# Row sums on every partition: a norm by one product on ones, a square root and a reciprocal of whole rows

## The chip, the cores and the metric

The kernel runs on one core of a Trainium2 chip. Its time is the device time of one execution in microseconds (us). Three executions of the kernel before took 1060.89, 1061.05 and 1061.98 us; the median is 1061.05 us. The engines are named as in the profile: PE is the matrix engine (TensorE), PEld its weight loads, DVE is VectorE, ACT is ScalarE, POOL is GpSimd, and SP issues DMAs. DMAs are issued from SP's and from ACT's queue. PSUM is the memory that PE writes its products to, SBUF the working memory.

## The reference

One inference step of a two-layer decoder trunk on 1056 tokens: 1024 of a prompt and 8 sequences of 4 sample tokens. Layer 0 is an RG-LRU block, layer 1 an HGRN2 block; each is a norm, an input projection, a mixer and an output projection that is added to the input. At the end stands one more norm. The change touches only how the norm is computed:

```python
def _rmsnorm(x, gain):
    xf = x.astype(jnp.float32)
    y = xf * lax.rsqrt(jnp.mean(xf * xf, axis=-1, keepdims=True) + EPS)
    return (y * gain.astype(jnp.float32)).astype(x.dtype)

# _trunk, shortened
for i in range(DEPTH):          # DEPTH = 2
    ...                         # layer 0: _lru_layer, layer 1: _hgrn_layer; each begins with _rmsnorm(x, g_norm)
return _rmsnorm(x, final_gain), ...
```

D_MODEL is 1024, EPS is 1e-6, and all is float32. The norm of x1 is the one at the entrance of layer 1, the final norm is the one in the last line.

## The kernel before

**Layout.** The tokens lie along the free dimension and the 1024 features along the partitions, in 8 blocks of 128 features. The sum of squares of a token is therefore a sum over partitions and over the 8 blocks. All large products are made of three products of parts (`mm3`, lines 243 to 245): each operand is split into a high and a low part, and high x high, high x low and low x high are added up in PSUM.

**Layer 0 and the norm of x1.** The tokens are cut into 3 chunks of 352. `out_last` computes the last part of layer 0's output projection, for each chunk 8 blocks m: a product on PE, an addition of the residual on DVE (line 698), a DMA, a square on ACT (line 430), and an addition of the square to an accumulator on POOL (line 433). After the 8 blocks of a chunk comes `norm`. It multiplies the accumulator, as weights, with a column of ones (`norm_sum`, line 277), three products of at most 128 tokens each, which leaves the sums with one token per partition. DVE scales them and adds EPS (line 445), POOL raises them to the power -0.5 (line 447), DVE makes a diagonal matrix of them (lines 448 and 451), and a product of a matrix of ones with that diagonal (line 453) brings the 352 factors as rows to all 128 partitions, in PSUM. `scaled_parts` multiplies each of the 8 blocks with its gain and with these rows (line 458, DVE), copies the high part (line 459, ACT) and subtracts it for the low part (line 323, DVE, or POOL for every fourth block). The first products of layer 1 (`first1`) read these parts: chunks 0 and 1 of two weight blocks first, chunk 2 of both last. Their first work on ACT is a Tanh (lines 714 and 718).

**The end of layer 1 and the final norm.** The output is finished in three pieces of 424, 376 and 256 tokens (`OUT`). For each piece and each of 8 blocks m: a product (9 matmuls), an addition on DVE (line 1724) that frees one of 3 PSUM banks, a square on ACT (line 1726), and for the first two pieces an addition to the accumulator on POOL (line 1735). Each piece's norm is worked off during the next piece: before block RM = 3 the sums (`summed`: `norm_sum`, then `roots` on DVE, POOL and DVE, lines 1664 to 1675), before block SM = 6 the product that spreads them (`spread`, line 1681) and then `finish`. `finish` multiplies each block with its gain and the factors. For the first piece DVE does all 8 blocks in one instruction each (line 1701), reading the factors from PSUM. For the others ACT copies the factors to SBUF (line 1694), ACT multiplies three blocks with the gain (line 1698) and POOL multiplies these with the copied factors (line 1699), while DVE does the other five from PSUM. Each block is written out by a DMA (line 310), in turn from SP's and ACT's queue.

For the last piece the sum over partitions is taken directly on PE: the accumulator of blocks 0 to 3 and then the squares of blocks 4 to 7 are each multiplied with the column of ones. Then come six products that nothing reads (line 1739), `roots`, `spread` and `finish`.

**What sets the order.** Each of the two layers collects all its instructions in a `Flow` with an engine, an estimated duration, what it reads and writes, and a priority. `Flow.run` plans the order of each engine's instructions from these estimates in turns, forwards and backwards, takes the best plan by its own estimate and writes the instructions in that order; for layer 0 a random search over the first 60 us is put on top. An instruction marked `both` is planned to wait for POOL where POOL is at work. So an edit of one instruction or one estimate can change the order elsewhere in the same layer. `hg` is a ring of PSUM banks, `xbs` a ring of three SBUF tiles of 384 columns.

Of the kernel before, what the change touches and what calls it, by code (L numbers as in the profile page):

```python
# [14 lines left out]
F32 = mybir.dt.float32  # L15
# [15 lines left out]
CUT = 2  # L31
SPOTS, SPOTS0, SPOTS1 = (6, 9, 0, 2), (2, 5, -1, -1), (1, 5, 9, 13, 17, 20)
K2 = 8 - K1
RM, SM = 3, 6
# [177 lines left out]
def tile_trunk(ctx: ExitStack, tc: tile.TileContext, xT, prm, hc, w0, wg, wo0, w1, wo1, s_in,  # L212
# [46 lines left out]
    smn = [0]  # L259

# [35 lines left out]
    with ExitStack() as l0:  # L296
# [18 lines left out]
        def dve(n, emit, r, w, prio=5, both=False):  # L315
            fl.add("DVE", 0.13 + 0.0011 * n, emit, r, w, prio, both=both)
# [118 lines left out]
        def norm(acc, own=None):  # L435
# [18 lines left out]
            return bc[:, :CH], bk  # L454

# [192 lines left out]
        def out_last(src):  # L648
# [42 lines left out]
            for c in range(NCH):  # L691
                acc = next(xbs)
                rows = []
                for i, m in enumerate(ms[c]):
                    ps, pk = product(blocks[m].get, ycols(c) + xcols(c)[:3], 1)
                    x, xk = spare[c][m]
                    dma(x, src[m][:, chunk(c)], ((2, m, c),), (xk,), 3)
                    dve(CH, lambda x=x, ps=ps: V.tensor_tensor(x, ps[:, :CH], x, op=ALU.add), (pk, xk), (xk,), 0)
                    dma(x1d[m][:, chunk(c)], x, (xk,), (("x1d", m, c),), 3)
                    squares(i, x, xk, acc)  # L700
                    rows.append((m, x, xk))
                bc, bk = norm(acc)
                for m, x, xk in rows:
                    scaled_parts(c, m, x, xk, bc, bk, pc("g1", m), ("P",), G if m % 4 == 3 else V, 4)
# [222 lines left out]
    with ExitStack() as l1:  # L927
# [728 lines left out]
        accs, sqs, dgs, sb = cycle(spare[:2]), cycle(spare[2:5]), cycle(spare[5:7]), spare[7]  # L1656
        nr2 = cycle([(fixed(f"nr2{i}", [128, 4], F32, p1), ("nr2", i)) for i in range(2)])

        def roots(n, sums, ready):

            r, rk = next(nr2)
            dg, dk = next(dgs)
            f, u = n // 128, n % 128
            dve(4, lambda: V.memset(r, 1.0), (), (rk,), 0)
            srcs = [(slice(i, i + 1), s[:w]) for i, (s, (_, w)) in enumerate(zip(sums, spans(n)))]
            for q, src in srcs:
                dve(4, lambda q=q, src=src: V.tensor_scalar(r[:src.shape[0], q], src, 1.0 / D, EPS, op0=ALU.mult, op1=ALU.add),
                    ready, (rk,), 0)
            w = len(srcs)
            fl.add("POOL", 0.85, lambda: G.tensor_tensor(r[:, :w], r[:, :w], mhalf[:, :w], op=ALU.pow), (rk,), (rk,), 0)  # L1670
            dve(128 * f, lambda: V.tensor_tensor(dg[:, :128 * f].rearrange("p (i n) -> p i n", i=f),
                                                 ident[:, None, :].to_broadcast([128, f, 128]),
                                                 r[:, :f, None].to_broadcast([128, f, 128]), op=ALU.mult), (rk,), (dk,), 0)
            if u:
                dve(u, lambda: V.tensor_scalar(dg[:, 128 * f:n], ident[:, :u], r[:, f:f + 1], None, op0=ALU.mult), (rk,), (dk,), 0)
            return dg[:, :n], dk

        def spread(n, dg, dk, main):

            bc, bk = next(hg)  # L1680
            fl.add("PE", 0.002 * n, lambda: T.matmul(bc[:, :n], ones, dg, start=True, stop=True), (dk,), (bk,), 0, main=main)
            return bc[:, :n], bk

        def summed(acc, ak, n):
            s, sk = next(hg)
            sums = [s[:, i:i + 1] for i in range(4)]
            fl.add("PE", 0.7, lambda: norm_sum(sums, acc, n, True, True), (ak,), (sk,), 0, main=True)
            return roots(n, sums, (sk,))

        def finish(a, n, bc, bk):  # L1690
            q = slice(a, a + n)
            own = KD - 3 if a else KD
            if a:
                act(n, lambda: S.copy(sb[0][:, :n], bc), (bk,), (sb[1],), 0)
            for k in (*range(own, KD), *range(own)):
                x, xk = x2[k][:, q], ykeys(Y2 + k, a, n)
                if k >= own:
                    act(n, lambda x=x, k=k: S.activation(x, x, AF.Copy, scale=pc("gf", k)), xk, xk, 1)
                    pool(n, lambda x=x: G.tensor_tensor(x, x, sb[0][:, :n], op=ALU.mult), (sb[1], *xk), xk, 1)
                else:  # L1700
                    dve(n, lambda x=x, k=k: V.scalar_tensor_tensor(x, x, pc("gf", k), bc, op0=ALU.mult, op1=ALU.mult), (bk, *xk), xk, 1)
                dma(yT[k][:, q], x, xk, (), 1, n / 2, S if k % 2 else Q)

        for a, n in OUT:
# [32 lines left out]
        spin, wk = next(mm)  # L1737
        for _ in range(6):
            fl.add("PE", 0.22, lambda: T.matmul(spin[:, :128], ones, ones, start=True, stop=True), sumk, (wk,), 0)
        finish(a, n, *spread(n, *roots(n, sums, sumk), False))  # L1740
# [72 lines left out]
```

## Time and profile before

| | |
|---|---|
| median of three runs | 1061.05 us (1060.89 to 1061.98) |
| the profiled execution: its own time | 1062.88 us |
| the profiled execution: its span, first to last instruction | 1061.1 us |
| mean granted TensorE clock | 0.995 |
| DVE busy | 843.7 us (80%) |
| ACT busy | 588.2 us (55%) |
| POOL busy | 542.0 us (51%) |

The profile comes from one execution. Every line of a timeline gives the start, the duration, the engine, the source line, the operation, the output and its inputs by the program's names, and the shape; a bracket gives idle time before it and who ended it. A line "x3" merges three instructions, and its duration is then that of the group. "PEclk" and "granted clock" give the clock that the matrix engine was granted, as a share of full speed. In the chain that ended last, a row is a piece of time that belongs to one engine and line, and the pieces do not overlap. An instruction's recorded duration includes a part that overlaps with its neighbour, so that two instructions in a row start closer together than one lasts.

### The profile page before, as it was taken

How to read it: one execution, taken by the hardware profiler on the slowest of the kernel's cores; microseconds unless marked ns; L12 is line 12 of the kernel's file. 1: busy time of each engine (PE TensorE's matmuls, PEld its weight loads, DVE VectorE, ACT ScalarE, POOL GpSimd, SP SyncE). 2: the span in 40 equal slices, each digit the busy share in tenths (PEclk: the TensorE clock that was granted, in tenths of full speed). 3: DMA queues.
4: the chain of work that ended last, by engine and by line, in shares of the span. 5: the costliest groups of instructions: out<-in, count | busy, mean ns of one | idle time of the engine just before them, and what ended most of it. 6: DMA issues, size and time to landing. Idle time of an engine off the chain costs nothing.

```text
span 1061.1 us, 25695 instructions
## 1 busy us (share of the span) xinstructions
PE 1051.4 (99%) x9972; PEld 1025.8 (97%) x9972; DVE 843.7 (80%) x1677; ACT 588.2 (55%) x1329; POOL 542.0 (51%) x604
## 2 busy tenths in 40 slices
PE   9999999999999999999999999999999999999997
PEld 9999999999999999999999999999999999999996
DVE  7999996888888689265799988978879797994435
ACT  6568656867675875243354474646464645652323
POOL 3425443444444455555677656555555565642544
PEclk9999999999999999999999999999999999999997
DMA  9201112123742685440210131312121212354204
GB/s 301 64 26 45 54 51 74 57 61 108 240 150 61 182 287 165 133 130 28 73 51 30 44 101 45 101 37 89 44 83 53 85 58 74 113 181 156 85 1 164
DMA packets 70121, 103.07 MB, mean 97 GB/s; under 512 B 9200, under 2 KB 51184, under 8 KB 70000
## 3 DMA queue, kind: packets, MB, share of 16 engines
q1 hardware_dynamic: 67696, 98.67, 29.9%
q10 hardware_dynamic: 2304, 2.77, 0.8%
q8 instruction: 78, 1.28, 0.5%
q14 instruction: 43, 0.35, 0.1%
HBM read 71.05 MB, written 25.49 MB: 91 GB/s over the span
## 4 chain that ended last, share of the span: by engine, by line
PE 89%; DVE 7%; POOL 1%; DMA 1%; issue 1%; ACT 0%; POOLq 0%; ACTq 0%; DVEq 0%
PE mm L243 24%; PE mm L244 24%; PE mm L245 24%; PE hg L567 1%; PE hg L1052 1%; PE hg L1161 1%; PE hg L1271 1%; DVE R L1368 1%; PE hg L1217 1%; PE hg L243 1%; PE hg L244 1%; PE hg L245 1%; PE hg L1273 1%; DMA wraw<-in_w_dram 1%; DVE tmp L1368 1%
## 5 line engine op out<-in xcount | busy, mean ns | idle before, releaser
L243 PE MATMUL mm<-xh,whi 128*128 128x352 f32 (+1 forms) x1143 | 358.8, 314 | 0.0
L245 PE MATMUL mm<-xh,wlo 128*128 128x352 f32 (+1 forms) x1143 | 353.4, 309 | 0.0
L244 PE MATMUL mm<-xl,whi 128*128 128x352 f32 (+1 forms) x1143 | 353.4, 309 | 0.0
L323 POOL TENSOR_TENSOR wlo<-wraw,whi 128x256 fp32r<-128x256 f32 (+3 forms) x184 | 203.2, 1121 | 178.7 <-ACT whi L378 79.9
L244 PEld LDWEIGHTS mm<-xl,whi 128*128 128x128 f32 x1143 | 215.3, 188 | 1.5
L243 PEld LDWEIGHTS mm<-xh,whi 128*128 128x128 f32 x1143 | 215.0, 188 | 1.5
L245 PEld LDWEIGHTS mm<-xh,wlo 128*128 128x128 f32 x1143 | 215.0, 188 | 0.0
L499 DVE SCALAR_TENSOR_TENSOR k<-xb,prm_sb,k 128x352 f32<-128x352 f32 (+2 forms) x144 | 90.0, 636 | 10.9 <-ACT k L496 7.7
L243 PE MATMUL mm<-t,whi 128*128 128x264 f32 (+1 forms) x306 | 89.4, 292 | 0.0
L244 PE MATMUL mm<-t,whi 128*128 128x264 f32 (+1 forms) x306 | 87.8, 287 | 0.0
L245 PE MATMUL mm<-t,wlo 128*128 128x264 f32 (+1 forms) x306 | 87.6, 286 | 0.0
L1501 DVE TENSOR_TENSOR k<-mm,k 128x264 f32<-128x264 f32 x144 | 60.2, 426 | 20.6 <-PE mm L245 17.5
L323 POOL TENSOR_TENSOR wlo<-R,whi 128x256 fp32r<-128x256 f32 x64 | 60.0, 957 | 24.7 <-ACT whi L1428 24.7
L582 POOL TENSOR_TENSOR k<-X 128x352 f32<-128x352 f32 x36 | 43.9, 1228 | 47.8 <-DVE R L583 38.2
L378 ACT CAST whi<-wraw 128x512 fp32r<-128x512 f32 (+2 forms) x83 | 46.1, 574 | 30.0 <-PE mm L244 15.7
L243 PEld LDWEIGHTS mm<-t,whi 128*128 128x128 f32 x306 | 57.7, 188 | 0.2
L245 PEld LDWEIGHTS mm<-t,wlo 128*128 128x128 f32 x306 | 57.8, 189 | 0.0
L244 PEld LDWEIGHTS mm<-t,whi 128*128 128x128 f32 x306 | 57.7, 189 | 0.0
L1428 ACT CAST whi<-wraw 128x512 fp32r<-128x512 f32 x52 | 32.1, 619 | 36.3 <-PE mm L245 16.8
L243 PE MATMUL mm<-yh,whi 128*128 128x352 f32 x153 | 50.0, 327 | 0.0
L245 PE MATMUL mm<-yh,wlo 128*128 128x352 f32 x153 | 49.4, 323 | 0.0
L244 PE MATMUL mm<-yl,whi 128*128 128x352 f32 x153 | 49.4, 323 | 0.0
(479 smaller groups left out, 2640.9 us busy)
## 6 DMA issues: line engine op xcount, KB each, us to landing
wraw<-in_w_dram SPq DMA_DIRECT2D x90, 256.0 KB, 2.8
wraw<-in_wo_dram SPq DMA_DIRECT2D x34, 192.0 KB, 2.6
si<-in_s_in_dram SPq DMA_DIRECT2D x8, 512.0 KB, 3.6
out_ss_out_dram<-si SPq DMA_DIRECT2D x8, 512.0 KB, 2.6
R<-in_w_dram SPq DMA_DIRECT2D x15, 256.0 KB, 2.6
sg<-x1b SPq DMA_DIRECT2D x21, 176.0 KB, 3.0
x<-sg SPq DMA_DIRECT2D x21, 176.0 KB, 1.9
R<-td SPq DMA_DIRECT2D x72, 44.0 KB, 2.0
```

Of the source, the lines that this page charges most:

```text
L243: T.matmul(out, wh, xh, start=first, stop=False)
L244: T.matmul(out, wh, xl, start=False, stop=False)
L245: T.matmul(out, wl, xh, start=False, stop=last)
L323: emit = lambda: e.tensor_tensor(b, x, a.bitcast(F32), op=ALU.subtract)
L378: act(m, lambda hi=hi, raw=raw, m=m: S.copy(hi[:, :m], raw[:, :m]), rk, (hk,), prio)
L499: dve(u, lambda src=src, dst=dst, sh=sh, k=k: V.scalar_tensor_tensor(dst, sh(src, k), pc("cw", 12 * k + m), dst, op0=ALU.mult, op1=ALU.add ...
L567: fl.add("PE", 0.62, lambda ps=ps, i=i, c=c: T.matmul(ps[:96, :CH], gs[:, i, :], ST[:96, chunk(c)], start=True, stop=True), (("gs",), *((" ...
L582: pool(CH, lambda x=x, a=a, b=b: G.tensor_tensor(x, a.bitcast(F32), b.bitcast(F32), op=ALU.add), (ak, bk), (xk,), 3)
L1052: T.matmul(ps[32 * j:32 * j + 32, n * w:n * w + w], B[:, o:o + 32], q(slice(o, o + 32)), start=True, stop=True, tile_position=(0, 32 * j))
L1368: dve(n, lambda: V.tensor_tensor(o, a, b, op=op), r, (w,), prio, True)
L1428: act(512, lambda: S.copy(hi, raw), (rk,), (hk,), 2)
L1501: dve(QT, lambda: V.tensor_tensor(o[0], z[0], u[0], op=ALU.add), (z[1], u[1]), (o[1],), 0)
```

## The change

For the norm of x1 (`norm_row` in place of `norm`, in `out_last` only; the first norm of layer 0 keeps `norm`) and for the final norm, the accumulator is now the moving operand of one product with a 128x128 matrix of ones. That leaves the sum of each token in every one of the 128 partitions, as a row in PSUM. ACT takes the square root of the whole row, with 1/D as scale and EPS as bias, and writes it to SBUF. DVE takes the reciprocal of the whole row in place. The scalings then read the factors from that SBUF row. The small products with a column of ones, the POOL power, the diagonal matrix and the product that spreads it go, and so do the ACT copy in `finish` and the six products that nothing reads. For the last piece the accumulator and the four squares are each multiplied with the matrix of ones, 256 columns wide. `finish` of a piece now follows its sums at once, before block 3; SM is gone. DVE's scalings in `finish` are marked `both`.

```diff
-RM, SM = 3, 6
+RM = 3
+TL = 1.3
...
+    epsc = const.tile([128, 1], F32, name="eps")
+    V.memset(epsc, EPS)
...
+        def norm_row(acc, o, ok):
+
+            a, ak = acc
+            ps, pk = next(hg)
+            fl.add("PE", 0.62, lambda: T.matmul(ps[:, :CH], ones, a[:, :CH], start=True, stop=True), (ak,), (pk,), 0)
+            act(CH, lambda: S.activation(o[:, :CH], ps[:, :CH], AF.Sqrt, bias=epsc, scale=1.0 / D), (pk,), (ok,), 0, TL)
+            dve(CH, lambda: V.reciprocal(o[:, :CH], o[:, :CH]), (ok,), (ok,), 0, more=1.2)
+            return o[:, :CH], ok
...
-                bc, bk = norm(acc)
+                bc, bk = norm_row(acc, *next(xbs))
...
+        def roots(n, ps, pk):
+
+            dg, dk = next(dgs)
+            act(n, lambda: S.activation(dg[:, :n], ps, AF.Sqrt, bias=epsc, scale=1.0 / D), (pk,), (dk,), 0)
+            fl.add("DVE", 0.13 + 0.0047 * n, lambda: V.reciprocal(dg[:, :n], dg[:, :n]), (dk,), (dk,), 0)
             return dg[:, :n], dk
...
         def summed(acc, ak, n):
             s, sk = next(hg)
-            sums = [s[:, i:i + 1] for i in range(4)]
-            fl.add("PE", 0.7, lambda: norm_sum(sums, acc, n, True, True), (ak,), (sk,), 0, main=True)
-            return roots(n, sums, (sk,))
+            fl.add("PE", 0.0018 * n, lambda: T.matmul(s[:, :n], ones, acc[:, :n], start=True, stop=True), (ak,), (sk,), 0, main=True)
+            return roots(n, s[:, :n], sk)
...
-            if a:
-                act(n, lambda: S.copy(sb[0][:, :n], bc), (bk,), (sb[1],), 0)
...
-                    pool(n, lambda x=x: G.tensor_tensor(x, x, sb[0][:, :n], op=ALU.mult), (sb[1], *xk), xk, 1)
+                    pool(n, lambda x=x: G.tensor_tensor(x, x, bc, op=ALU.mult), (bk, *xk), xk, 1)
                 else:
-                    dve(n, lambda x=x, k=k: V.scalar_tensor_tensor(x, x, pc("gf", k), bc, op0=ALU.mult, op1=ALU.mult), (bk, *xk), xk, 1)
+                    dve(n, lambda x=x, k=k: V.scalar_tensor_tensor(x, x, pc("gf", k), bc, op0=ALU.mult, op1=ALU.mult), (bk, *xk), xk, 1, True)
...
                 if a and m == RM:
-                    dg = summed(*prev[:2], prev[3])
-                if a and m == SM:
-                    finish(*prev[2:], *spread(prev[3], *dg, True))
+                    finish(*prev[2:], *summed(*prev[:2], prev[3]))
...
                     if m == 4:
-                        sums = [(next(hg)) for _ in spans(n)]
-                        sumk = [k for _, k in sums]
-                        sums = [s[:, :1] for s, _ in sums]
-                        fl.add("PE", 0.3, lambda acc=acc, n=n, sums=sums: norm_sum(sums, acc, n, True, False), (ak,), sumk, 0)
-                    fl.add("PE", 0.3, lambda sq=sq, n=n, m=m, sums=sums: norm_sum(sums, sq, n, False, m == KD - 1), (sk, *sumk), sumk, 0)
+                        ps1, pk1 = next(hg)
+                        fl.add("PE", 0.5, lambda acc=acc, n=n: T.matmul(ps1[:, :n], ones, acc[:, :n], start=True, stop=False), (ak,), (pk1,), 0)
+                    fl.add("PE", 0.5, lambda sq=sq, n=n, m=m: T.matmul(ps1[:, :n], ones, sq[:, :n], start=False, stop=m == KD - 1),
+                           (sk, pk1), (pk1,), 0)
...
-        spin, wk = next(mm)
-        for _ in range(6):
-            fl.add("PE", 0.22, lambda: T.matmul(spin[:, :128], ones, ones, start=True, stop=True), sumk, (wk,), 0)
-        finish(a, n, *spread(n, *roots(n, sums, sumk), False))
+        finish(a, n, *roots(n, ps1[:, :n], pk1))
```

More of the change, by code (lines that the diff above doesn't have):

```diff
@@ L313, in act, with dve @@
             fl.add("ACT", 0.25 + 0.0007 * n + more, emit, r, w, prio)
-        def dve(n, emit, r, w, prio=5, both=False):
-            fl.add("DVE", 0.13 + 0.0011 * n, emit, r, w, prio, both=both)
+        def dve(n, emit, r, w, prio=5, both=False, more=0.0):
+            fl.add("DVE", 0.13 + 0.0011 * n + more, emit, r, w, prio, both=both)
         def pool(n, emit, r, w, prio=5):
@@ L1655, in tile_trunk @@
                 spare.append((o[:, a:a + 512], key))
[L1656 to L1661, printed above, removed]
+        accs, sqs, dgs = cycle(spare[:2]), cycle(spare[2:5]), cycle(spare[5:])
+        def roots(n, ps, pk):
             dg, dk = next(dgs)
[L1663 to L1675, printed above, removed]
@@ L1676, in roots @@
+            act(n, lambda: S.activation(dg[:, :n], ps, AF.Sqrt, bias=epsc, scale=1.0 / D), (pk,), (dk,), 0)
+            fl.add("DVE", 0.13 + 0.0047 * n, lambda: V.reciprocal(dg[:, :n], dg[:, :n]), (dk,), (dk,), 0)
             return dg[:, :n], dk
[L1678 to L1682, printed above, removed]
         def summed(acc, ak, n):
```

## Prediction

> **What bounds the kernel now.** I read the page first, then stages, then the chain that ended last, then the tail as a timeline.
>
> ```profile
> span 1061.1 us, 25695 instructions
> PE 1051.4 (99%) x9972; PEld 1025.8 (97%) x9972; DVE 843.7 (80%) x1677; ACT 588.2 (55%) x1329; POOL 542.0 (51%) x604
> ```
>
> By stages (columns: span; length; busy us of PE, PEld, DVE, ACT, POOL; granted clock; DMA share; GB/s):
>
> ```profile
> 435.00:490.00 55.00, 55.00 (x347) 54.58 (x345) 26.54 (x55) 17.51 (x37) 24.44 (x25) 1.00 0.31 101
> 1029.50:1047.70 18.20, 18.20 (x128) 17.61 (x128) 12.88 (x34) 8.21 (x17) 10.59 (x13) 1.00 0.28 102
> 1050.00:1052.00 2.00, 1.92 (x9) 1.92 (x10) 0.32 (x2) 0.53 (x2) 0.65 (x2) 0.50 1.01 362
> ```
>
> Where the norm of x1 runs (435 to 490) PE is never idle, and DVE is busy half the time: there PE alone sets the time. In the last two pieces PE is full too, but DVE has only 18.20 - 12.88 = 5.32 us free. After 1047.7 PE no longer bounds; there is one chain of small steps, at half the clock. The chain that ended last gives what the norms take of PE:
>
> ```profile
> 441.13 0.51 PE hg L277 x6
> ...
> 460.60 0.59 PE hg L453 x2
> ...
> 489.91 0.51 PE hg L277 x6
> ...
> 1028.81 0.73 PE hg L277 x8
> ...
> 1034.39 0.71 PE mm L1681 x2
> ...
> 1041.37 0.55 PE hg L277 x6
> ...
> 1045.21 0.65 PE hg L1681 x2
> ```
>
> L277 are the small products with a column of ones (three groups in layer 0, the first and last shown, of 0.51 us each), L453 and L1681 the spreading products. The tail, from the last square on:
>
> ```profile
> 1049.61 0.42 ACT L1726 ACTIVATE sg<-sg 128x256 f32<-128x256 f32 x1 [0.48 <-DVE sg L1724]
> ...
> 1050.08 1.02 PE L277 MATMUL hg<-ones,sg 128*128 128x1 f32 x4 [0.45 <-ACT sg L1726]
> ...
> 1050.95 2.91 PE L1739 MATMUL mm<-ones 128*128 128x128 f32 x12
> ...
> 1051.37 0.70 POOL L1670 TENSOR_TENSOR nr<-nr,mhalf 128x2 f32<-128x2 f32 x1 [1.35 <-DVE nr L1667]
> 1052.10 0.42 DVE L1671 TENSOR_TENSOR sg<-ident,nr 128x256 f32<-128x256 f32 x1 [0.81 <-POOL nr L1670]
> ...
> 1053.65 1.06 PE L1681 MATMUL mm<-sg,ones 128*128 128x256 f32 x2
> 1054.75 0.37 ACT L1694 COPY sg<-mm 128x256 f32<-128x256 f32 x1 [4.19 <-PE mm L1681]
> 1055.16 0.48 DVE L1701 SCALAR_TENSOR_TENSOR ST<-ST,prm_sb,mm 128x256 f32<-128x256 f32 x1 [2.63 <-ACT sg L1694]
> 1055.20 2.09 POOL L1699 TENSOR_TENSOR sg<-sg 128x256 f32<-128x256 f32 x3 [3.13 <-ACT sg L1694]
> ...
> 1056.73 0.47 DVE L1701 SCALAR_TENSOR_TENSOR a<-a,prm_sb,mm 128x256 f32<-128x256 f32 x1
> ...
> 1057.66 0.41 SPq L310 DMA_DIRECT2D out_yT_dram<-sg  x1
> ```
>
> From the square's end (1049.61 + 0.42 = 1050.03) to the first scaling (1055.16) pass 5.13 us. The diagonal is ready at 1052.52, but the spreading product's matmul starts only at 1053.65: the idle products of L1739 hold PE. Then DVE scales five blocks until 1057.20 and POOL three until 1057.29, side by side; the last DMA issues at 1057.66.
>
> **The change part by part.** *PE in the full stages.* In each norm the spreading product gives way to a product of ones with the accumulator, of the same width and so the same price (0.59 at 352 columns, 0.71 at 424, 0.65 at 376). The small products go without replacement: 3 x 0.51 + 0.73 + 0.55 = 2.81 us. PE is full in these stages, so all of it counts. For the last piece four of the five small groups already ran after the last large product; five products of 256 columns take their place, and only the last of these is on the chain, counted below.
>
> *The chain of the last piece.* New: product, square root, reciprocal. The product's price lies between the one row of this width, 1.06 us at half the clock, and a row of 376 columns at the full clock, scaled by 256/376:
>
> ```profile
> 1045.05 0.79 PE L1681 MATMUL hg<-sg,ones 128*128 128x376 f32 x2
> L740 DVE RECIPROCAL smalls<-smalls x1: 214/214/214, 21.0 to 21.0; 128x12 f32<-128x12 f32 x1
> L773 DVE RECIPROCAL smalls<-smalls x1: 203/203/203, 124.4 to 124.4; 128x8 f32<-128x8 f32 x1
> L740 DVE TENSOR_SCALAR smalls<-smalls x12: 164/172/174, 5.2 to 58.0; 128x12 f32<-128x12 f32 x12
> ```
>
> That is 0.54 to 1.06; I take 0.75, nearer to the full clock, because five wide products keep PE busier than 20 products of one column. The square root is taken as a square of the same width, 0.42, plus 0.03 for its bias; as ends the copy's 0.37 and 0.6. A reciprocal of a row appears nowhere; its nearest rows have 12 and 8 elements. Their difference, 11 ns for 4 elements, gives 2.75 ns per element; all that exceeds 150 ns in the 8-element row gives 6.6; and 214 less a fixed 160 (the 172 of a plain instruction of 12 elements, less some 12) over 12 elements gives 4.5. I take 4.5, between the ends: 1.31 us for 256 (0.85 to 1.85), 1.85 for 376, 2.07 for 424. With three hand-overs of 0.05 (the square's end at 1050.03 to PE at 1050.08) the chain is 0.75 + 0.45 + 1.31 + 0.15 = 2.66 us, so 5.13 - 2.66 = 2.47 us are gained. The ends are 1.92 and 3.66 us, a gain of 3.2 or 1.5.
>
> *The scaling after it.* DVE's second large input moves from PSUM to SBUF. What that does beside POOL, in this trace:
>
> ```profile
> L458 DVE SCALAR_TENSOR_TENSOR sg<-sg,g,R x8: 580/581/1275, 43.1 to 75.1; 128x352 f32<-128x352 f32 x8
> ```
>
> ```profile
> 42.90 1.09 POOL L323 TENSOR_TENSOR xl<-R,xh 128x352 fp32r<-128x352 f32 x1 [2.69 <-ACT xh L459]
> 43.10 1.27 DVE L458 SCALAR_TENSOR_TENSOR sg<-sg,g,R 128x352 f32<-128x352 f32 x1
> ...
> 498.90 1.39 DVE L323 TENSOR_TENSOR xl<-sg,xh 128x352 fp32r<-128x352 f32 x3
> 498.99 1.81 POOL L720 TENSOR_SCALAR ST<-k,smalls 128x352 f32<-128x352 f32 x1 [1.40 <-ACT k L718]
> ...
> 502.45 0.63 POOL L720 TENSOR_SCALAR a<-k,smalls 128x352 f32<-128x352 f32 x1
> ```
>
> The same scaling, with both inputs in SBUF, takes 0.58 alone and 1.27 when it starts inside a POOL instruction: it ends 0.38 after POOL does (43.99). The other way round, a POOL instruction of 0.63 took 1.81 because three DVE subtractions from SBUF ran ahead until 500.29. So the two no longer run side by side: 2.04 + 2.09 = 4.13 us in place of 2.09. I take +1.9 (ends: 0, if they interleave as now, and 2.1). On this stands a rule of the Trainium skill, "SBUF — State Buffer", section "Who interferes with whom": a VectorE instruction with two SBUF inputs and a GpSimd instruction that reads SBUF lock each other out for a whole instruction. By that rule the scaling would take 4.1 us and the sum be -2.6; by the median of the eight rows, 581, it would stay near 2.1 and the sum be -4.7. The two stretched rows side with the rule.
>
> *DVE in the last two pieces.* The first row below holds what DVE and POOL do there on the small tile of sums (span; length; busy us of DVE, POOL), the others the last addition and what stands before it:
>
> ```profile
> 1029.50:1047.70 18.20, 2.38 (x12) 1.87 (x2) 1.00 0.28 102
> ```
>
> ```profile
> 1047.95 1.11 DVE L1701 SCALAR_TENSOR_TENSOR R<-R,prm_sb,hg 128x376 f32<-128x376 f32 x2
> 1048.98 0.42 DVE L1724 TENSOR_TENSOR sg<-mm,sg 128x256 f32<-128x256 f32 x1
> ```
>
> Out go DVE's 2.38 us and in come two reciprocals, 1.85 + 2.07 = 3.92: +1.5 us. The 13 scalings (8 of the first piece, 5 of the second) now read SBUF while POOL is busy 10.59 of 18.20 us. Free are 5.32 - 1.28 (PE's saving) - 1.5 = 2.5 us. At 0.24 us of waiting each, the 13 scalings need 3.1, so the last addition slips by 0.6. Ends: -1.0 (now it waits behind two scalings, 1047.95 to 1048.98, which can be moved) and, with the 0.69 of the row above for each, 13 x 0.69 - 2.5 = 6.5. I take 0.6 because the planner now reckons with the wait.
>
> *Without cost.* ACT's square roots need a table switch:
>
> ```profile
> L586 ACT ACT_TABLE_LOAD x12: 1283/1283/1283, 83.0 to 392.7; - x12
> ```
>
> Two to four of these 1.28 us loads come to the norm of x1 (17.51 us busy of 55 there), one to the final norm in the second piece, all beside a full PE; were a square to force the table back, the last chain would get 1.28. In layer 0 the scalings too read SBUF, and three reciprocals of 1.74 replace about 1 us of small steps each: DVE has 28 us free there. The ACT copy of a piece goes. DVE's scalings of the second piece no longer queue behind it. One more memset at the start is 0.06 us. A new plan can also move stalls elsewhere: PE idles 1061.1 - 1051.4 = 9.7 us in all, most of it in the tail, so little is left to win there; I take 0, with 1 us either way.
>
> *Sum.* -2.81 - 2.47 + 1.9 + 0.6 = -2.78 us. The profiled execution took 1062.88 us (span 1061.1), which becomes 1060.1; against the median of the runs, 1061.05, it is 1058.3.
>
> **The rivals.** *The lock does not bite.* If POOL and DVE interleave as now, +1.9 and +0.6 fall away: -5.3 us, 1055.8. For it: seven of eight rows at 0.58. Against: both overlaps above.
>
> *DVE takes up the gain.* The 13 scalings wait 0.4 us each: 5.2 - 2.5 = 2.7 in place of 0.6, and the end is at 1060.4, no change. For it: POOL is at work 58% of that stretch. Against: many scalings of the second piece can go behind the last addition.
>
> A plain addition at two widths, for the next rival:
>
> ```profile
> L1724 DVE TENSOR_TENSOR R<-mm,R 128x376 f32<-128x376 f32 x3 | 1.6, 549 | 3.4 <-PE mm L245 3.4
> L1724 DVE TENSOR_TENSOR sg<-mm,sg 128x256 f32<-128x256 f32 x3 | 1.3, 420 | 0.5 <-PE mm L245 0.5
> ```
>
> *The reciprocal is dearer.* If each element cost eight plain passes (plain: 549 ns at 376 columns, 420 at 256, so 1.07 ns per element), 8.6 ns, the three rows would cost 2.36, 3.4 and 3.8 us: +1.05 on the chain and +3.3 on DVE, 1062.6. Against: 12 elements would then take 263 ns, not 214. The Trainium skill says on the page "VectorE: DVE Perf Modes", section "First, the fixed hardware budget", that the reciprocal is an iterated divide with a repeat count of 8; if that means eight cycles an element, this is the time, and the trace's small rows do not bear it out.
>
> *Slower: the lock stalls PE.* If each of the 13 scalings meets POOL as at 43.10 (+0.69), DVE is 6.5 us late. An addition frees one of only three PSUM banks, so a delay beyond two products stops PE itself. The end comes at 1061.05 - 2.81 - 2.47 + 1.9 + 6.5 = 1064.2. It decides from (2.81 + 2.47 - 1.9 + 2.5)/13 = 0.45 us of waiting per scaling on.
>
> **How the numbers follow.** Of this kernel 0.2% is 2.1 us, about what its runs can tell from no change. Forecast 1058.3, its own range 1056.8 to 1060, chance 0.48 (0.35 of it faster by over 0.2%, 0.13 within). No lock: 0.16, faster. DVE takes up the gain: 0.14, within. Dear reciprocal: 0.07, within mostly (0.03 slower). Lock stalls PE: 0.15, slower. Faster 0.51, same 0.31, slower 0.18. The range runs from 1055.5 to 1062.7, leaving out the slower rival and the far ends of the first.
>
> **What would show it.** PE work on L277 from layer 1's end on gone and each x1 norm shorter by 0.5 us; from the last square to the first scaling 2.7 us; the last three POOL scalings starting about 2 us after DVE's first; DVE's reciprocals near 1.3, 1.85 and 2.07 us; the last addition no more than about 1.6 us after PE's last large product. The prediction is wrong if PE shows idle time before 1045, or if a table load stands between the last square and the last root.

## The result, and the profile after

The changed kernel takes 1067.66 us (median of four runs, 1067.41 to 1068.26); the kernel before took 1061.51 us (1060.89 to 1062.07) beside it. The ratio is 1.0059, with an interval of 1.0041 to 1.0076: slower by 0.6%, where 1058.3 us was forecast with a range up to 1062.7. The profiled execution took 1067.9 us with a span of 1066.1 us, 5.0 us more than before's 1061.1. The medians differ by 6.2 us: before's profiled execution, 1062.88 us, was 1.4 us longer than its median, so the traces show that much less.

Lines of the page of the changed kernel that answer to the first fence of the prediction:

```profile
span 1066.1 us, 25555 instructions
PE 1049.0 (98%) x9916; PEld 1022.1 (96%) x9916; DVE 863.7 (81%) x1652; ACT 596.3 (56%) x1338; POOL 535.2 (50%) x598
```

PE works 2.4 us less than before and yet idles 17.1 us in place of 9.7. Where, the windows say (columns as in the prediction: span; length; busy us of PE, PEld, DVE, ACT, POOL; granted clock; DMA share; GB/s). First the kernel before, then the changed one:

```profile
30.00:60.00 30.00, 29.22 (x180) 28.12 (x179) 29.18 (x76) 15.17 (x33) 10.44 (x16) 1.00 0.18 51
515.00:600.00 85.00, 83.95 (x1077) 81.54 (x1076) 81.56 (x157) 37.81 (x90) 55.99 (x56) 1.00 0.14 43
545.00:550.00 5.00, 5.00 (x74) 4.74 (x73) 4.96 (x11) 3.29 (x8) 1.85 (x2) 1.00 0.22 62
1024.00:1048.00 24.00, 24.00 (x166) 23.38 (x164) 15.42 (x39) 9.82 (x20) 13.92 (x15) 1.00 0.22 81
```

```profile
30.00:60.00 30.00, 28.15 (x174) 27.20 (x173) 28.50 (x77) 13.45 (x28) 9.91 (x13) 1.00 0.20 61
435.00:490.00 55.00, 55.00 (x340) 54.58 (x339) 30.72 (x45) 19.48 (x39) 24.68 (x23) 1.00 0.33 105
515.00:600.00 85.00, 82.00 (x1042) 79.74 (x1041) 80.05 (x150) 34.65 (x84) 49.02 (x51) 0.98 0.13 41
545.00:550.00 5.00, 4.47 (x88) 4.37 (x79) 5.00 (x10) 1.94 (x4) 0.74 (x1) 0.66 0.16 54
1024.00:1048.00 24.00, 22.57 (x132) 21.43 (x130) 14.43 (x21) 10.71 (x20) 13.32 (x12) 1.00 0.10 37
```

The norm of x1 (435 to 490) hides everything behind a full PE, as before. The new idle time lies at the start (30 to 60: 1.85 us in place of 0.78), where nothing was edited but a memset, at the start of layer 1 (515 to 600: 3.00 in place of 1.05), where nothing was edited at all, and in the last pieces (1.43 in place of 0); 2.6 us more lie behind 1048 (9.46 in place of 6.83), where PE no longer sets the time. In layer 1 the clock falls too: 0.66 over five microseconds, 5 x 0.34 = 1.7 us of work lost on top of 3.00 - 1.05 = 1.95 us of idling. The list of PE's waits from 490 to 600 has one large entry, and the timeline shows it:

```profile
PE hg L1064 <- DVE sg L1046: 2.5, 1, 2.5
...
544.33 0.76 PE L1064 MATMUL hg<-R,sg 128*32 128x32 f32 x64 [2.47 <-DVE sg L1046]
```

How late the changed kernel is can be followed by the start of the same instruction (the same run of the same line) in both traces, here in us after the kernel before, with the experiments below beside it. Each column is one profiled execution. The start of "final alone, old order" is the one of the kernel before but for a memset, and yet it is 0.85 us late, so differences under about 1 us mean nothing here.

| at us (before) | instruction of before | changed | x1 alone, old order | final alone, old order | both, old order | no search | final alone, new plan |
|---|---|---|---|---|---|---|---|
| 53.68 | ACT L531 | +2.26 | +0.09 | +0.85 | -0.21 | +2.28 | +0.29 |
| 443.24 | DVE L698 | +2.49 | +0.05 | +0.83 | -0.25 | +3.12 | +0.28 |
| 502.24 | ACT L718 | +1.73 | -1.65 | +0.81 | -2.07 | +3.19 | +0.25 |
| 656.56 | DVE L1501 | +5.75 | -1.32 | +0.87 | -1.76 | +3.38 | +2.58 |
| 1005.60 | DVE L1627 | +5.63 | -1.15 | +1.00 | -1.59 | +3.25 | +3.10 |
| 1048.98 | DVE L1724, the last addition | +5.60 | -1.24 | +4.36 | +1.63 | +3.25 | +3.10 |

The tail of the changed kernel, from the last square on, as a timeline:

```profile
1054.92 2.47 DVE L1691 SCALAR_TENSOR_TENSOR R<-R,prm_sb,sg 128x376 f32<-128x376 f32 x3
...
1055.44 0.42 ACT L1714 ACTIVATE sg<-sg 128x256 f32<-128x256 f32 x1 [0.30 <-PE hg L1719]
...
1056.11 0.59 PE L1719 MATMUL hg<-sg,ones 128*128 128x256 f32 x2
...
1057.44 0.47 ACT L1673 ACTIVATE sg<-hg,eps 128x256 f32<-128x256 f32 x1 [1.04 <-DVE R L1691]
1057.95 1.75 DVE L1674 RECIPROCAL sg<-sg 128x256 f32<-128x256 f32 x1
1059.74 1.05 DVE L1691 SCALAR_TENSOR_TENSOR ST<-ST,prm_sb,sg 128x256 f32<-128x256 f32 x1
1059.78 2.45 POOL L1689 TENSOR_TENSOR sg<-sg 128x256 f32<-128x256 f32 x3 [3.32 <-DVE sg L1674]
1060.71 2.20 DVE L1691 SCALAR_TENSOR_TENSOR R<-R,prm_sb,sg 128x256 f32<-128x256 f32 x3
1062.83 0.47 DVE L1691 SCALAR_TENSOR_TENSOR a<-a,prm_sb,sg 128x256 f32<-128x256 f32 x1
```

From the square's end (1055.86) to the first scaling (1059.74) pass 3.88 us, not 5.13 and not the 2.66 forecast. DVE's five scalings take 1059.74 to 1063.30, 3.56 us in place of 2.04: DVE and POOL now take turns. The other reciprocals (one of three in the norm of x1, and those of the first two pieces), and two of the five table loads that came with the roots (the first of four in the norm of x1, and the one of the final norm):

```profile
464.31 2.35 DVE L465 RECIPROCAL xb<-xb 128x352 f32<-128x352 f32 x1 [0.65 <-ACT xb L464]
...
1037.62 2.80 DVE L1674 RECIPROCAL sg<-sg 128x424 f32<-128x424 f32 x1 [2.58 <-ACT sg L1673]
...
1050.40 2.49 DVE L1674 RECIPROCAL sg<-sg 128x376 f32<-128x376 f32 x1
```

```profile
461.37 1.28 ACT L464 ACT_TABLE_LOAD   x1
...
1035.67 1.28 ACT L1673 ACT_TABLE_LOAD   x1
```

From 1.75 us at 256 columns to 2.80 at 424 is 1.05 us for 168 elements: 6.2 ns an element and some 0.15 us besides.

### The profile page after: what moved, and what is told of

It is laid out like the page before. It is cut to its first block, busy times and chain, and to the rows that moved or that the text cites. A ratio compares the mean times of both kernels' runs of the same rounds, so it can differ in the third digit from the quotient of the medians.

```text
span 1066.1 us, 25555 instructions
## 1 busy us (share of the span) xinstructions
PE 1049.0 (98%) x9916; PEld 1022.1 (96%) x9916; DVE 863.7 (81%) x1652; ACT 596.3 (56%) x1338; POOL 535.2 (50%) x598
## 3 DMA queue, kind: packets, MB, share of 16 engines
q8 instruction: 78, 1.28, 0.5%
## 4 chain that ended last, share of the span: by engine, by line
PE 47%; DVE 4%; POOL 0%; ACT 0%; issue 0%; DVEq 0%; POOLq 0%; ACTq 0%
PE mm L244 12%; PE mm L245 12%; PE mm L246 12%; PE hg L1064 1%; PE hg L1173 1%; PE hg L1283 1%; PE hg L1229 1%; PE hg L1285 1%; DVE R L1380 1%; DVE R L1691 1%; PE mm L1064 1%; DVE tmp L1380 1%; PE hg L1258 1%; PE hg L1327 0%; DVE sg L1674 0%; DVE R L1046 0%
## 5 line engine op out<-in xcount | busy, mean ns | idle before, releaser
L511 DVE SCALAR_TENSOR_TENSOR k<-xb,prm_sb,k 128x352 f32<-128x352 f32 (+2 forms) x144 | 92.8, 654 | 11.2 <-ACT k L508 7.8
```

The lines of the kernel that those rows point to most:

```text
L511: dve(u, lambda src=src, dst=dst, sh=sh, k=k: V.scalar_tensor_tensor(dst, sh(src, k), pc("cw", 12 * k + m), dst, op0=ALU.mult, op1=ALU.add ...
```

## The experiments

Two theories stood against each other. One: the new instructions themselves cost the time (reciprocals, and DVE and POOL locking each other out). The other: the new order of the whole plan costs it. To separate them, I gave the planner the old steps with their old durations, and only when it writes the instructions out does a step emit the new one (`nothing` emits none); so every other instruction keeps its place. This is called the old order below. The norm of x1 (`X1`), the first two pieces (`MID`) and the last piece (`LAST`) have a switch each: "col" is the old form, "sbuf" the new one; with all three at "col" the kernel is the one before. `RECIP` says whether the reciprocals are emitted. In the first two runs `MID` and `LAST` were still one switch, `FIN`. The rows of the norm of x1 lie in another tile here (`R`, not `xbs`). The diff sets old steps of the final norm beside those that stand at their places; it is cut, and the kernels keep both in functions of their own:

```diff
+X1, MID, LAST, RECIP = "col", "col", "col", True
...
-            fl.add("POOL", 0.85, lambda: G.tensor_tensor(r[:, :w], r[:, :w], mhalf[:, :w], op=ALU.pow), (rk,), (rk,), 0)
+            fl.add("POOL", 0.85, lambda: S.activation(dg[:, :n], ps, AF.Sqrt, bias=epsc, scale=1.0 / D), (rk,), (rk,), 0)
...
-            dve(128 * f, lambda: V.tensor_tensor(dg[:, :128 * f].rearrange("p (i n) -> p i n", i=f),
...
+                dve(n // 128 * 128, lambda: V.reciprocal(box.get("bc", dg)[:, :n], dg[:, :n]), (rk,), (dk,), 0)
...
-                dve(u, lambda: V.tensor_scalar(dg[:, 128 * f:n], ident[:, :u], r[:, f:f + 1], None, op0=ALU.mult), (rk,), (dk,), 0)
+                dve(n % 128, nothing, (rk,), (dk,), 0)
...
-            fl.add("PE", 0.002 * n, lambda: T.matmul(bc[:, :n], ones, dg, start=True, stop=True), (dk,), (bk,), 0, main=main)
+            fl.add("PE", 0.002 * n, nothing, (dk,), (bk,), 0, main=main)
```

**The new norm of x1 alone, old order.**

```diff
-X1, MID, LAST, RECIP = "col", "col", "col", True
+X1, MID, LAST, RECIP = "sbuf", "col", "col", True
```

> The new norm of x1 alone, put into the order of the kernel before: the planner is given the old steps, and at their places the new instructions are written (the product of ones at the old sums, the square root at the old power, the reciprocal at the old diagonal, nothing at the old spread), so every other instruction of every engine keeps its place. Theory A (the loss comes from the new order that the planner chose, not from the new instructions): the three sums of 0.51 us go, so 1.5 us faster than before, about 1060.0; no startup loss, no stall at the start of layer 1. Theory B (the new instructions do it: scalings from SBUF hold POOL up at the end of layer 0 and so the start of layer 1): 2 to 3.5 us slower than before, 1063.5 to 1065, with own_gate about 2.5 us later against PE.

Measured 1060.17 us, ratio 0.9984 (0.9974 to 0.9993). In the table above it is 1.65 us early after the norm of x1, and keeps 1.2 to 1.3 to the end: three times 0.51 us of small products were forecast. This is what the theory of the new order expected: this part of the change is a gain when nothing else moves.

**The new final norm alone, old order.**

```diff
-X1, MID, LAST, RECIP = "col", "col", "col", True
+X1, MID, LAST, RECIP = "col", "sbuf", "sbuf", True
```

> The new final norm alone in the order of the kernel before, by the same method; layer 0 as before. Both theories: nothing changes up to 1024 us. The reciprocals cost 6.2 ns per element as in the changed kernel (1.75, 2.5 and 2.8 us). Theory A: the two sums go from PE (1.28 us) and the chain from the last square to the first scaling falls from 5.1 to about 3.5 us, of which the lock on the last scalings gives 2 us back: about 1060.5, a gain of 0.5 to 1. Theory B (DVE cannot carry the reciprocals and the locked scalings): PE idles after 1035 and the end is 1 to 3 us later, 1062 to 1064.

Measured 1065.86 us, ratio 1.0031 (1.0019 to 1.0042): here the new instructions do cost, as the other theory said, and more than it said. DVE's first scalings of the first piece in the trace, with POOL's addition beside the second, the reciprocals of the first two pieces before and after them, and the last stage by windows:

```profile
1033.00 2.80 DVE L1720 RECIPROCAL sg<-sg 128x424 f32<-128x424 f32 x1 [0.31 <-ACT sg L1718]
1036.58 0.65 DVE L1761 SCALAR_TENSOR_TENSOR R<-R,prm_sb,sg 128x424 f32<-128x424 f32 x1
1036.97 1.12 POOL L1802 TENSOR_TENSOR R<-R,a 128x376 f32<-128x376 f32 x1 [2.45 <-ACT a L1792]
...
1037.15 1.40 DVE L1761 SCALAR_TENSOR_TENSOR ST<-ST,prm_sb,sg 128x424 f32<-128x424 f32 x1
...
1046.42 2.50 DVE L1720 RECIPROCAL sg<-sg 128x376 f32<-128x376 f32 x1 [0.27 <-ACT sg L1718]
```

```profile
1024.00:1050.00 26.00, 23.96 (x152) 22.53 (x151) 19.25 (x27) 11.51 (x22) 13.25 (x15) 1.00 0.19 68
```

A scaling of 424 columns takes 0.65 us alone and 1.40 where it meets POOL. PE now idles 2.04 of 26 us, and the last addition slips from +1.00 to +4.36 us: in the old order the final norm makes PE wait, as the rival "the lock stalls PE" said, if not at its price. The 13 scalings of the first two pieces take 11.87 us in sum in place of 8.20, so 0.28 us more each; the rival had 0.69.

**The same two halves, planned anew.** Here the changed kernel is taken and one half is undone, steps and all; the planner then makes its own order. First the final norm is undone (the whole end of layer 1 is before's; the diff is cut):

```diff
-RM = 3
+RM, SM = 3, 6
...
-                    finish(*prev[2:], *summed(*prev[:2], prev[3]))
+                    dg = summed(*prev[:2], prev[3])
+                if a and m == SM:
+                    finish(*prev[2:], *spread(prev[3], *dg, True))
```

> The new norm of x1 alone, planned anew as in the changed kernel (layer 0 in the changed kernel's own order), the final norm as before. Theory A: 2 us lost in the first 60 us and some 3.5 at the start of layer 1, hardly anything of it given back: 1065 to 1067. Theory B: the same time as the new norm of x1 in the old order, within 1 us.

Measured 1064.64 us, 1.0020 (1.0010 to 1.0029): the gain of 1.7 us becomes a loss of 2.1 once the plan is made anew. By the instructions of the table its trace is 1.66 us late at 443, 0.94 at 502, 2.26 at 656 and 2.07 at the last addition: it too loses at the start, and some at the start of layer 1, whose steps are those of the kernel before.

Then the norm of x1 is undone:

```diff
-                bc, bk = norm_row(acc, *next(xbs))
+                bc, bk = norm(acc)
```

> The new final norm alone, planned anew as in the changed kernel, the norm of x1 and the whole of layer 0 in the order of before. Theory A: the startup is that of before; if the stall at the start of layer 1 belongs to layer 0's order the time is 1060 to 1062, if it belongs to layer 1's own new order 1063 to 1065. Theory B: the time of the new final norm in the old order, within 1 us.

Measured 1064.62 us, 1.0024 (1.0014 to 1.0033). Layer 0 is then the old one, and it is on time until 502 (+0.25), but loses 2.3 us at the start of layer 1, some 490 us ahead of anything that was edited. So the large wait belongs to layer 1's own new order. There this trace has the same wait, and the clock falls behind it:

```profile
541.71 0.76 PE L1064 MATMUL hg<-R,sg 128*32 128x32 f32 x64 [2.05 <-DVE sg L1046]
```

```profile
541.00:543.00 2.00, 0.76 (x64) 0.68 (x65) 2.00 (x4) 0.98 (x2) 0.11 (x1) 0.87 0.34 109
543.00:545.00 2.00, 1.99 (x68) 1.96 (x69) 2.00 (x5) 0.41 (x1) 0.75 (x1) 0.50 0.09 31
545.00:550.00 5.00, 5.00 (x30) 5.00 (x30) 4.68 (x12) 2.43 (x6) 0.35 (x1) 0.91 0.02 5
```

The new plan gives that back in the last pieces, where it stays at +3.10 and the old order slipped by 3.4 us. So for the final norm the two orders cost about the same, at different places.

**The lock and the reciprocals apart.** In the old order again, the reciprocal is written to `bc`, a PSUM tile, DVE scales from there, and an ACT copy serves POOL as before ("psum"):

```diff
-X1, MID, LAST, RECIP = "col", "sbuf", "sbuf", True
+X1, MID, LAST, RECIP = "col", "psum", "psum", True
...
+                act(n, lambda: S.copy(sb[0][:, :n], bc), (bk,), (sb[1],), 0)
```

> The new final norm in the old order, as in the run of the final norm alone, except that DVE writes the reciprocals into PSUM: DVE's scalings read them there, and ACT copies them to SBUF for POOL as the kernel before did. The reciprocals stay as long. Theory L (the lock between DVE's scalings from SBUF and POOL makes the loss of 3.2 us): most of it goes, within 1 us of the kernel before; the last five scalings take 2.0 us again, not 3.6. Theory R (the reciprocals on DVE make it): no more than 1.5 us better than the run with SBUF, so 1.5 us or more over the kernel before.

Measured 1062.04 us, 1.0002 (0.9993 to 1.0012): 0.0029 below the form with SBUF rows, 3 us. The second scaling of the first piece, which took 1.40 us, again with a POOL addition beside it, and the last stage:

```profile
1035.86 1.00 POOL L1805 TENSOR_TENSOR R<-R,a 128x376 f32<-128x376 f32 x1 [2.50 <-ACT a L1795]
...
1036.03 0.65 DVE L1764 SCALAR_TENSOR_TENSOR ST<-ST,prm_sb,mm 128x424 f32<-128x424 f32 x1
```

```profile
1024.00:1050.00 26.00, 25.14 (x157) 23.03 (x155) 19.31 (x32) 12.83 (x25) 13.45 (x15) 1.00 0.23 83
```

Next, with SBUF rows, the reciprocals are left out, so the scalings use the square roots themselves and the last output is another one:

```diff
-X1, MID, LAST, RECIP = "col", "sbuf", "sbuf", True
+X1, MID, LAST, RECIP = "col", "sbuf", "sbuf", False
```

> The new final norm in the old order with SBUF rows, and the three reciprocals left out: the scalings use the square roots themselves, so the last output is not the reference's. Theory L: only the 1.8 us of the last reciprocal is gained on the chain, the end stays 1 to 1.5 us over the kernel before. Theory R: the stretch before the end catches up too: the last large product is no later than in the kernel before, and the end is 1 to 3 us under it.

Measured 1060.72 us, 0.9988 (0.9979 to 0.9998): 0.0043 below, 4.5 us, of which 1.75 are the last reciprocal on the chain. So taking away either the lock or the reciprocals regains about what this norm loses. Each removal relieves DVE in the same stretch; whether the two gains add up was not tried.

**All of the change in the old order.**

```diff
-X1, MID, LAST, RECIP = "col", "col", "col", True
+X1, MID, LAST, RECIP = "sbuf", "sbuf", "sbuf", True
```

> All new instructions of the change, both norms, issued in the order that the kernel before has. If the two norms add up and the new order is what is left, the ratio to before is 0.9984 x 1.0031 = 1.0015 (about 1063.7 us), and the changed kernel's 1.0059 less this, 0.0044 or 4.7 us, is the price of the order. If instead the new instructions of the two norms disturb each other, it comes out near 1.006 with the old order too.

Measured 1063.99 us, 1.0018 (1.0009 to 1.0028). The halves add up (0.9984 x 1.0031 = 1.0015), and the changed kernel's other 0.0041, 4.4 us, is the order, with the tiles and banks that came with it. By the table the new order costs 2.7 us at the start, 1.1 in the norm of x1 and 3.4 at the start of layer 1, and it gives 3.3 back in the last pieces. In the old order PE is as full as in the kernel before at the start and at the start of layer 1:

```profile
30.00:60.00 30.00, 29.54 (x181) 28.44 (x180) 29.16 (x76) 15.05 (x33) 10.45 (x16) 1.00 0.17 50
515.00:600.00 85.00, 83.94 (x1080) 81.52 (x1079) 81.72 (x151) 37.82 (x90) 57.53 (x57) 1.00 0.14 44
```

**The order alone, without any edit of an instruction.** The random search over the first 60 us with another seed:

```diff
-        rng = Random(1)
+        rng = Random(2)
```

> The kernel before with another random seed (2 for 1) of the search over the first 60 us; not one instruction differs, only the order at the start. Theory A (the new order costs): the time moves by 1 to 3 us, in the first 60 us, upwards more likely than down. Theory B: it stays within 0.5 us.

Measured 1067.28 us, 1.0056 (1.0040 to 1.0072). No instruction differs, the planned end is the same 507.60 us as with the old seed, and it costs as much as the whole change. Its trace, of the slowest of four executions (1066.43 to 1070.13 us), is 3.9 us late at 53.68 and 6.3 at 443. Why the changed kernel's start is another one at all can be read from the planner: it compares the searched plan with the one before the search by their planned ends and, at a tie, keeps the first. In the kernel before the search won, 507.60 against 507.78. In the changed kernel both end at 505.26, so the search's result is thrown away. The next kernel is the kernel before with no search:

```diff
-            fl.run(SEARCH, 60.0)
+            fl.run(0, 60.0)
```

> The kernel before with the random search over the first 60 us of layer 0 left out: no instruction differs, only the order. The changed kernel's planner prefers its unsearched plan, because the searched one, 1.1 us earlier at the search's own check point by the planner's figures, has the same planned end, 505.26, and a tie goes to the first; the matrix engine's order at the start of the changed kernel is the one that this kernel has too. If the lost search is what makes the changed kernel late at the start, this one is about 2 us late at 60 us and its ratio is about 1.002. If the added memset or the new operations downstream do it, it is on time at 60 us and the ratio is 1.000.

Measured 1064.59 us, 1.0028 (1.0019 to 1.0037), and at 53.68 it is 2.28 us late, as the changed kernel is (2.26). The windows of the two kernels, first with the other seed, then with no search:

```profile
30.00:60.00 30.00, 27.77 (x171) 26.68 (x171) 28.18 (x67) 15.08 (x32) 11.04 (x14) 1.00 0.20 58
```

```profile
30.00:60.00 30.00, 27.63 (x168) 26.30 (x168) 28.88 (x77) 13.19 (x28) 11.17 (x13) 1.00 0.19 58
```

So the changed kernel has its late start because a tie in the planner's comparison leaves it the unsearched plan; in the kernel before, that plan costs 3.0 us in all. That the searched plan would have been better is not said by this. The other way round, the changed kernel with the searched plan taken at the tie:

```diff
-        return min(best, self.plan(key), key=lambda g: g[0])
+        return min(self.plan(key), best, key=lambda g: g[0])
```

> The changed kernel with one thing altered: of two plans with the same planned end the searched one is taken. If the search is worth on the chip what it is worth in the kernel before, about 2 us come back: ratio to before near 1.004, and no lateness at 60 us. If the planner's figures do not tell on the chip (another random seed cost the kernel before 5 us at the same planned end), it can come out anywhere between 1.001 and 1.010.

Measured 1073.1 us, 1.0098 (1.0078 to 1.0118): slower still. The planner counts 1.1 us less for the searched plan to its check point near 80 us, the chip takes 3.9 us longer at 54 (+6.15 in place of +2.26). One wait does most of it, and the clock halves after it:

```profile
36.19 0.66 PE L244 MATMUL mm<-xh,yh 128*128 128x352 f32 x1 [3.20 <-DVE sg L539]
```

```profile
36.00:42.00 6.00, 5.81 (x18) 5.31 (x19) 4.11 (x11) 2.88 (x7) 1.11 (x3) 0.50 0.41 136
```

**What is worth keeping.** The new norm of x1, and the new form for the last piece alone, with its factors in PSUM, all in the old order:

```diff
-X1, MID, LAST, RECIP = "col", "col", "col", True
+X1, MID, LAST, RECIP = "sbuf", "col", "psum", True
```

> All in the old order: the new norm of x1, and of the final norm only the last piece in the new form, with its reciprocals written to PSUM; the first two pieces keep the old form, so that DVE has no more to do there. Both theories: 1.5 us from the norm of x1, and on the last chain 5.1 us become 3.2 (product 0.75, root 0.47, reciprocal 1.75, hand-overs), 1.9 us: 3.4 us under the kernel before, about 0.997 of it.

Measured 1061.01 us, 0.9990 (0.9981 to 1.0000), no better than the norm of x1 alone, where about 0.997 was expected. The timeline of its tail says why:

```profile
1049.41 1.28 ACT L1718 ACT_TABLE_LOAD   x1
1050.71 0.47 ACT L1718 ACTIVATE sg<-hg,eps 128x256 f32<-128x256 f32 x1
```

No earlier root of the final norm has fetched the table now, so the load stands in the last chain, after the last square. The next kernel takes a root of a single value that nothing reads, in the second and third piece:

```diff
+            def power(w=w):
+                G.tensor_tensor(r[:, :w], r[:, :w], mhalf[:, :w], op=ALU.pow)
+                S.activation(early, epsc, AF.Sqrt)
```

> As the kernel with the new norm of x1 and the new norm of the last piece, but ScalarE takes the root of one value during the second and third piece, so that the table is there when the last root comes. If the load is what cost that kernel its gain, no load stands in the last chain, from the last square's end to the first scaling pass 3.3 us in place of 4.55, and the time is 1061.0 - 1.28 = 1059.7 us (ratio 0.998). If the scaled copies and squares that follow force another table back, the load stands there again and the time is about 1061.

Measured 1059.57 us, 0.9979 (0.9969 to 0.9989): faster than both kernels, by 0.2% against the one before. That it beats the new norm of x1 alone (0.9974 to 0.9993) the intervals do not show. The load stands in the second piece, and the last chain takes 3.49 us, from the square's end at 1048.55 to the first scaling:

```profile
1028.54 1.28 ACT L1706 ACT_TABLE_LOAD   x1
...
1048.13 0.42 ACT L1802 ACTIVATE sg<-sg 128x256 f32<-128x256 f32 x1 [0.48 <-DVE sg L1800]
...
1048.60 0.70 PE L1778 MATMUL hg<-sg,ones 128*128 128x256 f32 x2 [0.40 <-ACT sg L1802]
1049.34 0.47 ACT L1725 ACTIVATE sg<-hg,eps 128x256 f32<-128x256 f32 x1 [0.25 <-PE hg L1778]
1049.84 1.76 DVE L1728 RECIPROCAL mm<-sg 128x256 f32<-128x256 f32 x1 [1.41 <-ACT sg L1725]
1051.64 0.37 ACT L1763 COPY sg<-mm 128x256 f32<-128x256 f32 x1 [1.83 <-DVE mm L1728]
1052.04 0.48 DVE L1771 SCALAR_TENSOR_TENSOR ST<-ST,prm_sb,mm 128x256 f32<-128x256 f32 x1 [0.44 <-ACT sg L1763]
1052.09 2.09 POOL L1769 TENSOR_TENSOR sg<-sg 128x256 f32<-128x256 f32 x3 [3.55 <-ACT sg L1763]
```

## Why the prediction was wrong

**The step that failed** is "A new plan can also move stalls elsewhere: PE idles 1061.1 - 1051.4 = 9.7 us in all, most of it in the tail, so little is left to win there; I take 0, with 1 us either way." The argument bounds only what a new plan can win. What it can lose has no such bound: DVE is over 95% busy at both places (29.18 of 30 us, and 81.56 of 85), so a delay of DVE there can reach PE, and in the changed kernel it did. The order cost 4.4 us; with the two norms in the old order the same change costs 1.9 us. That is still no gain of 2.8: a second step, the 0.6 us for DVE in the last two pieces, failed as well (below). Why the planner's estimates did not see the wait of 2.47 us is open. The prediction's own sign of being wrong, PE idle before 1045, could not tell: the kernel before already idles 2.9 us ahead of 1048, the changed one 7.6.

**The forecast's terms against the changed kernel's trace**, in us against before, from the table of lateness and the tail:

| stage | forecast | measured | from |
|---|---|---|---|
| start, to 443 | 0 | +2.5 | +2.49 |
| norm of x1 | -1.5 | -0.8 | 1.73 - 2.49 (old order: -1.7) |
| start of layer 1 | 0 | +3.9 | 5.63 - 1.73 |
| last pieces | -1.28 + 0.6 = -0.7 | 0.0 | 5.60 - 5.63 |
| last addition to first scaling | -2.5 | -1.0 | 4.58 - 5.60 |
| last scalings | +1.9 | +1.5 | 3.56 - 2.04 |
| last writes | 0 | -1.1 | the span's 5.0 less the sum of these |

The sum itself was set against the wrong execution. The 5.13 us of the old chain are read from the profiled one, whose clock is 0.50 in the tail and 0.995 on average, and the gain is then taken off the median. Among the executions recorded beside the experiments, those of the kernel before with a mean granted clock of 0.999 took 1061.0 to 1061.4 us, those with 0.995 took 1062.7 to 1063.9. That a shorter tail makes the difference, so that there was less to gain in the median execution, is likely, but no trace here shows it.

**PE in the full stages: right for the norm of x1** (1.5 forecast, 1.7 measured in the old order). For the final norm the saving of 1.28 us went under in PE's waits: the last pieces are no shorter.

**The last chain: the mechanism right, the size off.** 3.88 us stand against 2.66. In the old order (final norm alone) the chain takes 3.08 us, from 1054.31 to 1057.39: there the dearer reciprocal is nearly the whole miss, and the other 0.8 come with the new order. In the changed kernel, of the missing 1.22, the reciprocal took 1.75 in place of 1.31; the root started 0.74 us after its product's end (1056.70 to 1057.44), and the profile puts that to DVE's stretched scalings of the second piece; the product, 0.59 for 0.75, began 0.25 us after the square in place of 0.05. Which of the root's semaphores held it was not tried. An earlier root alone would not have helped, though: DVE works on the last scaling of the second piece until 1057.92, and the reciprocal starts at 1057.95. The reciprocal's 6.2 ns an element lie inside the ends (2.75 to 6.6) near the upper; I had taken 4.5, from rows of 12 and 8 elements, where the fixed part is nearly the whole time. The rival of eight passes had 8.6: the Trainium skill's repeat count of 8 ("VectorE: DVE Perf Modes", section "First, the fixed hardware budget"), read as eight cycles an element, is not what these rows show.

**The lock: right.** 1.5 us stand against 1.9; the two engines' whole work is not stacked, they alternate, and only the first three of DVE's five scalings meet POOL. That it is the lock, and not the reciprocal, that stretches the scalings is shown by the kernel with PSUM factors (0.65 in place of 1.40, with POOL at work beside both). This agrees with the Trainium skill, "SBUF — State Buffer", section "Who interferes with whom".

**DVE in the last two pieces: undersized.** The two reciprocals cost 5.29 us where 3.92 were reckoned. In the old order the last addition slips by 4.36 - 1.00 + 1.28 = 4.6 us, not 0.6. The wait per scaling was not the fault: 0.28 us against 0.24. With the measured scalings and reciprocals the prediction's own sum gives 3.66 + 1.37 - 2.5 = 2.5 us, so 2.1 remain. Most likely they are free time of DVE that the sum counted in full and that the old order could not use; this was not tried. PE waits as in the rival "the lock stalls PE", but not by its 0.69 a scaling. In the changed kernel the new plan holds the slip to about 1.3 (the saving of 1.28 used up). That fits the reason given, that "the planner now reckons with the wait"; the same planning cost more elsewhere.

**Without cost: right for the table loads.** Four loads come to the norm of x1, where PE is full until 490 and idles 0.3 us from 490 to 515, one comes to the final norm in the second piece, and no square forces the table back. That the last chain is free of it hangs on the earlier pieces' roots, as the kernel with only the last piece showed.

## What to carry to other kernels

Where a planner writes the whole order, an edit is two changes, its own instructions and a new order; measure the edit with the old order pinned before judging it, and give the new order a range from the same kernel planned with another seed (here up to 6 us, 0.6%, with the planned end unchanged). Take the cost per element of a row-wide operation from rows of that length, and price the engine that it fills, not only the chain that it shortens. A table load that a first use hides can come out on the critical chain once that first use is dropped; here a single dummy activation moved it off again.

## What the hardware showed beside

A wait of PE of 2 us cost almost twice itself here. After waits of 2.05 and 2.47 us, with 64 products of 32 columns behind them, the clock falls, and both times the same is lost: 2 x 0.13 + 2 x 0.50 + 5 x 0.09 = 1.7 us with the new final norm alone, 5 x 0.34 = 1.7 us in the changed kernel. After the wait of 3.20 us it is at least 6 x 0.50 = 3.0 us. Waits of 0.53 us behind the same 64 products in the kernel before, of 1.07 us (at 34 and at 1040) in the changed kernel and of 1.23 us (at 31) in the one with no search left the clock at 1.00. Where between 1.23 and 2.05 us the edge lies, no run shows. The Trainium skill, "TensorE: Matmul & The Clock Gate", section "Part 1: The HAM clock gate (the "warmup" mystery)", has half the clock after an idle window of about 3.4 us, and windows of that length; 3.4 us at half the clock are the 1.7 us lost here, so the length agrees, but these waits were shorter than a window and yet the clock fell.

The searched and the unsearched order differ by 1.1 us in the plan and by 3.9 us, the other way, on the chip. Which of the planner's estimates is to blame was not tried.
